# An attention layer on one core: output weights' sums made beside stage two's seven products, and residual additions moved from GpSimd to accumulating DMAs and VectorE

## The chip, the cores and the metric

The kernel runs on one core of a Trainium2 chip. The core has a matrix engine (TensorE, in the profile PE, with PEld for its weight loads) and three engines for elementwise work: VectorE (DVE), ScalarE (ACT) and GpSimd (POOL). A fifth, SyncE (SP), issues most of the DMAs; its queue is served in order. Each engine runs its instructions in program order and waits on semaphores for data from the others. The metric is the device time of one execution in microseconds, as the median of several runs.

## The reference

One pre-norm layer of a vision-like trunk, with 2048 tokens of width 1024 on a grid of 64 columns, 16 heads of 64, all in float32:

```python
h = rmsnorm(x, norm_0)
q, k, v, gate = split(h @ w_in_0, 4)                 # w_in_0: 1024 x 4096
o = neighbourhood_attention(q, k, v, rpb_0)          # 8 x 16 window, bias per head
x = x + (o * silu(gate)) @ w_out_0                   # w_out_0: 1024 x 1024
out = rmsnorm(x, norm_f)
```

The layer norm's factor is the inverse root of the mean square of each token; the same holds for the last norm. The window is cut at the edges of the grid.

## The kernel before

**Products.** TensorE multiplies 128x128 blocks with moving tiles of 128x512. To keep float32 accuracy, each operand is split into a high part (made on ScalarE by a copy to the matrix format) and a low part (the difference, made on VectorE), and a product is three matmuls: high by high, high by low, low by high. Where a 2x2 arrangement of blocks is at hand, the kernel uses Strassen's scheme with seven products in place of eight. It needs sums of quarters of both operands (S1 to S4 on one side, T1 to T4 on the other); a product is then 12 matmuls (4 blocks of the inner dimension by 3).

**Stages.** Stage one makes the norm's statistics, v for the first half of the tokens and q, k, gate for them by seven products. Stage two does the same for the second half: first the value projections (`values_of`, called by `pair`, line 834: 16 tiles of 24 matmuls), then nine units of seven products (`seven_products`, line 405; the order of the seven is 1, 6, 2, 7, 5, 4, 3). Then come 32 steps of attention (scores, softmax, transposes, values), with further projections and the first six tiles of output rows fed in between. Last come the other ten tiles of output rows, in five pairs by seven products (`rows_product` and `rows_by_seven`, lines 1440 and 1479), with the residual, the last norm and the stores.

**The output weights' sums.** For the last part the kernel needs T1 to T4 of `w_out`. They are made in stage two's value projections: for each of four row blocks k, `out_rows(k)` (line 886) issues four loads of 256 KB into OW, `out_sum` forms one difference on VectorE, and `out_split` makes high and low part of it and puts two stores to DRAM (`wod`) in the list of later stores. They stand in the table of `pair` calls (lines 919 to 937) as steps between two groups of matmuls. The same calls hold `w` (splits of the value weights), `lw` (loads of value weights, line 533), `v` (values out of PSUM), `block`, `t123`, `t4` and `form` (the other operands of stage two).

**What sets the order.** The program is written in the order in which each engine gets its instructions; there is no scheduler. `store(key, lag, f)` puts a piece of work into a list, and `due(n)`, called with each matmul, lets it out after `lag` matmuls. `ahead` in stage two makes high and low parts six products ahead. In the seven products of stage two a function `also(n, i)` is called after product i of the unit n (n counts up to 0 for the last unit). In the last part `LEAD` says how many products ahead the high and low parts are made, and `todo` says after which product of `seq` loads, sums and parts are issued. The weight tiles of value unit 1 use the buffers of unit 0's, and the landing tiles `raw` go round over six buffers.

**PSUM in the last part.** In a pair (n0, n1) of row tiles, products 1 and 2 share one bank, 6, 7 and 4 a second, 5 and 3 a third. Product 1 is copied out to `p` (U[m, 1]). After product 6, `u` = bank + p is the part of (n0, 1); after product 7, `u` = bank + p is that of (n1, 1); and p goes into (n1, 0). So product 7 waits until u of product 6 has read the bank, product 4 until u of product 7 has, and product 3 until the addition y of product 5 has. `add_rows` (line 1224) adds the bank to what stands in RES and leaves the square sums to ScalarE. What stands in RES for (n0, 1), (n1, 1) and (n1, 0) is u or p with the residual tile already added, by three additions on GpSimd (lines 1464 and 1468). The residual tiles are loaded by `load_rest_of` on SP's queue into `rbp` (three buffers) or `qp`.

Of the kernel before, what the change touches and what calls it, by code (L numbers as in the profile page):

```python
# [71 lines left out]
def build(ctx, tc, x, xr, xt, wg, rpb, last, w_out, n0, nf, masks, out):  # L72
# [728 lines left out]
    def stage_two():  # L801
# [8 lines left out]

        def also(n, i):
# [72 lines left out]
        OW = {}  # L884

        def out_rows(k):
            def g():
                for q, (r_, c_) in quarters.items():
                    OW[q] = kp([128, 960], F32, "ow")[:, :512] if r_ else ep([128, 512], F32, "ow")
                    nc.sync.dma_start(OW[q], w_out[(4 * r_ + k) * 128:(4 * r_ + k + 1) * 128, c_ * 512:c_ * 512 + 512])  # L890
            return g

        def out_sum(k, f):
            def g():
                a, b = {"T1": ("B12", "B11"), "T3": ("B22", "B12"), "T2": ("B22", "B11"), "T4": ("B21", "B22")}[f]
                o = OW[{"T1": "B11", "T3": "B12", "T2": "B22", "T4": "B21"}[f]]
                nc.vector.tensor_tensor(o, OW[a], OW[b], OP.subtract)
            return g

        def out_split(k, f):  # L900
            def g():
                o = OW[{"T1": "B11", "T3": "B12", "T2": "B22", "T4": "B21"}[f]]
                h, l = ev([128, 512], F32R, "oh"), ev([128, 512], F32R, "ol")
                split_to(h, l, o, None)
                for i, s in enumerate((h, l)):
                    store(("ow", f, k, i), 5, lambda i=i, s=s: nc.sync.dma_start(wod[f][:, k, i], s.bitcast(F32)))
            return g

# [7 lines left out]
        def o(k, *fs):  # L916
            return [(out_sum if f[0] == "+" else out_split)(k, "T" + f[-1]) for f in fs]

        pair(0, (8, 9), both(w(0, 3), lambda: spread_rstd(3)), both(lw(1, 0), block("B12", x12, 0, 1)),
             both(block("B12", x12, 2, 3), out_rows(0)), block("B22", x22, 0, 1))  # L920
        pair(0, (10, 11), both(v(0, 8, 9), block("B22", x22, 2, 3)), t123(0), t123(1), both(lw(1, 1), *o(0, "+1")))
# [4 lines left out]
        pair(1, (13,), both(v(1, 12), form("T2", x11, 2), *o(1, "=3")), both(form("T2", x11, 3), *o(1, "+2")), both(*o(1, "=2", "+4")),  # L926
             both(*o(1, "=4")))
        pair(1, (14,), both(v(1, 13), form("T3", x22, 0), out_rows(2)), form("T3", x22, 1), both(), both(*o(2, "+1")))
        pair(1, (15,), both(v(1, 14), lambda: ahead(-9, -1), *o(2, "=1", "+3")), both(form("T3", x22, 2), *o(2, "=3")),
             both(form("T3", x22, 3), *o(2, "+2")), both(*o(2, "=2", "+4")))  # L930
        pair(1, (8,), both(v(1, 15), lambda: ahead(-8, -1), *o(2, "=4")), both(t1(0), out_rows(3)), t1(1), lambda: ahead(-7, -1))
        pair(1, (9,), both(v(1, 8), t1(2), *o(3, "+1")), both(t1(3), *o(3, "=1")), both(lambda: ahead(-6, -1), *o(3, "+3")),
             both(form("T4", x21, 0), *o(3, "=3")))
        pair(1, (10,), both(v(1, 9), form("T4", x21, 1), *o(3, "+2")), both(form("T4", x21, 2), *o(3, "=2")),
             both(form("T4", x21, 3), *o(3, "+4")), both(*o(3, "=4")))
# [288 lines left out]
    def add_rows(n, j, ps):  # L1224
# [213 lines left out]

    def rows_product(m, P):
# [17 lines left out]
        elif P == 2:  # L1457
            add_rows(n0, 0, B[m, 2])
        elif P in (6, 7):
            U[m, P] = xp([128, 512], F32, "u")  # L1460
            nc.vector.tensor_tensor(U[m, P], B[m, P], U[m, 1], OP.add)
            to = (n0, 1) if P == 6 else (n1, 1)
            r = RES.pop(to)
            nc.gpsimd.tensor_tensor(U[m, P], U[m, P], r, OP.add)
            RES[to] = U[m, P]
            if P == 7:
                r = RES.pop((n1, 0))
                nc.gpsimd.tensor_tensor(U[m, 1], U[m, 1], r, OP.add)
                RES[n1, 0] = U[m, 1]
        elif P == 5:  # L1470
            add_rows(n1, 1, B[m, 5])
        elif P == 4:
            add_rows(n1, 0, B[m, 4])
            finish(n1)
        else:
            add_rows(n0, 1, B[m, 3])
            finish(n0)

    def rows_by_seven():
        for f, (r, c) in plain_of.items():  # L1480
            TF[f] = [(woh[4 * r + k, c], wol[4 * r + k, c]) for k in range(4)]
        E, LEAD = 3, 4
        seq = [(m, P) for P in (1, 2) for m in range(E)]
        seq += [(0, 6), (1, 6), (0, 7), (0, 5), (1, 7), (0, 4), (1, 5), (0, 3), (1, 4), (2, 6), (1, 3), (2, 7), (2, 5), (2, 4), (2, 3)]
        seq += [(m, P) for m in range(E, len(PAIRS)) for P in order7]
# [13 lines left out]
        for i, m, j, k in ((1, 0, 1, 0), (2, 1, 1, 0), (4, 0, 0, 1), (5, 0, 1, 1), (6, 1, 0, 1), (7, 1, 1, 1), (9, 2, 0, 1), (9, 2, 1, 0),  # L1499
                           (11, 2, 1, 1)):  # L1500
            on(i, load_rest_of, m, j, k)
        for m in range(E, len(PAIRS)):
            s = seq.index((m, 1))
            for d, f in ((-9, "A21"), (-8, "A22"), (-7, "A11"), (-6, "A12")):
# [214 lines left out]
```

## Time and profile before

| what | value |
|---|---|
| median of 3 runs | 1055.19 us (1054.54 to 1059.93) |
| the profiled execution's own time | 1056.66 us |
| its span, first to last instruction | 1054.9 us |
| mean granted clock of TensorE | 0.997 |
| DMA moved | 205.30 MB, mean 195 GB/s |
| stage two's value projections | about 326 to 420 us |
| stage two's seven products | about 420 to 590 us |
| the last five pairs of row tiles | 949.7 to 1048.9 us |

The span is the time on the core from the first to the last instruction; the execution's own time is a little longer. On the page, busy times of engines overlap. Rows of a timeline give start, duration, engine, line, operation, output and input, and in brackets the idle time before it and what ended that. In rows of windows each engine has its busy time and its count of instructions, then come the clock granted to TensorE (1.00 is full speed), the share of DMA engines' time and GB/s.

### The profile page before, as it was taken

Reading aid. Unit: us, or ns where it says so; the run is one execution under the profiler, and the core shown is the slowest. Engines: PE = TensorE matmul, PEld = TensorE weight load, DVE = VectorE, ACT = ScalarE, POOL = GpSimd, SP = SyncE. Lnnn points to the kernel's source line nnn. Section 1 sums busy time; section 2 is a strip of 40 time slices with the busy share of each in tenths; the row PEclk is TensorE's granted clock in tenths of the full one; section 3 lists DMA queues with packets and bytes.
Section 4 is the critical chain, followed back from the end, with each engine's and each line's share of the span. In section 5 each row is a group of like instructions: output and inputs, shape, how many; then the busy total and the mean of one; then the engine's idle time right before and its main releaser. Section 6 shows DMA issues by size and latency. Waiting matters only on the chain.

```text
span 1054.9 us, 20328 instructions
## 1 busy us (share of the span) xinstructions
PE 1039.0 (98%) x7256; PEld 850.1 (81%) x7256; DVE 743.2 (70%) x1601; ACT 558.4 (53%) x1305; POOL 278.1 (26%) x357
## 2 busy tenths in 40 slices
PE   9999999999999989999999999999999999999987
PEld 6888888887888868888888788888888787888776
DVE  5385657778897847655565666667777788777996
ACT  7545323344344435333333477788887877673433
POOL 0000231321221000000000477765565432420331
PEclk9999999999999999999999999999999999999999
DMA  9633444452637568434243787868877689899442
GB/s 312 226 100 100 140 145 129 134 151 96 195 119 211 168 230 293 126 108 132 80 145 121 237 246 218 260 199 279 249 237 247 186 269 312 277 352 354 148 172 80
DMA packets 133213, 205.30 MB, mean 195 GB/s; under 512 B 12216, under 2 KB 56504, under 8 KB 133112
## 3 DMA queue, kind: packets, MB, share of 16 engines
q1 hardware_dynamic: 132680, 203.61, 60.7%
q8 instruction: 57, 0.93, 0.4%
q10 hardware_dynamic: 432, 0.40, 0.1%
q14 instruction: 44, 0.36, 0.1%
HBM read 145.24 MB, written 58.72 MB: 193 GB/s over the span
## 4 chain that ended last, share of the span: by engine, by line
PE 89%; DVE 7%; issue 1%; ACT 1%; DMA 1%; POOL 0%; ACTq 0%; DVEq 0%
PE pp L438 36%; PE pv L562 12%; PE s L1063 8%; PE o L1170 8%; PE py L1451 7%; PE ph L1148 4%; PE pp L384 2%; PE po L1372 2%; PE po L1374 2%; PE pp L386 2%; PE pp L382 2%; PE po L1376 2%; DMA raw<-in_wg_dram 1%; DVE l L521 1%; DVE y L1291 1%
## 5 line engine op out<-in xcount | busy, mean ns | idle before, releaser
L438 PE MATMUL pp<-h,f 128*128 128x512 f32 x672 | 217.6, 389 | 0.0
L1077 ACT ACTIVATE x<-x,st 128x360 f32<-128x360 f32 (+5 forms) x256 | 151.2, 592 | 24.6 <-DVE st L1071 24.6
L438 PEld LDWEIGHTS pp<-h,f 128*128 128x128 f32 x672 | 126.1, 188 | 26.5 <-DVE f L421 0.3
L438 PE MATMUL pp<-t,f 128*128 128x512 f32 x558 | 141.7, 389 | 0.1
L1091 POOL TENSOR_SCALAR x<-x,st 128x480 f32<-128x480 f32 (+5 forms) x192 | 114.4, 613 | 94.1 <-DVE st L1082 91.8
L438 PE MATMUL pp<-l,f 128*128 128x512 f32 x336 | 130.7, 389 | 0.0
L458 POOL TENSOR_TENSOR tmp<-tmp,rb 128x512 f32<-128x512 f32 x36 | 58.4, 1622 | 271.1 <-DVE tmp L456 235.7
L1071 DVE CUSTOM_DVE_ANT_0 x<-s,em 128x360 f32<-128x360 f32 (+5 forms) x256 | 123.0, 535 | 0.3 <-PE s L1063 0.3
L438 PEld LDWEIGHTS pp<-t,f 128*128 128x128 f32 x558 | 104.7, 188 | 22.3 <-DVE u L451 0.6
L1031 POOL TENSOR_TENSOR em<-e,mk 128x264 f32<-128x264 f32 (+3 forms) x64 | 50.8, 825 | 266.2 <-DMA mk<-in_masks_dram 252.7
L421 DVE TENSOR_TENSOR f<-raw,f 128x512 fp32r<-128x512 f32 x105 | 76.5, 728 | 37.4 <-ACT f L420 37.3
L1063 PE MATMUL s<-kt,q 64*128 64x480 f32 (+5 forms) x512 | 95.5, 488 | 0.1
L562 PE MATMUL pv<-wh,h 128*128 128x512 f32 x256 | 90.0, 397 | 4.4 <-ACT wh L542 4.4
L1170 PEld LDWEIGHTS o<-pta,vt 120*64 120x64 f32 (+2 forms) x1792 | 80.9, 137 | 14.4 <-DVE st L1071 13.6
L562 PE MATMUL pv<-wl,h 128*128 128x512 f32 x256 | 89.8, 396 | 0.3 <-DVE wl L545 0.3
L562 PE MATMUL pv<-wh,l 128*128 128x512 f32 x256 | 89.5, 395 | 0.0
L1170 PE MATMUL o<-pta,vt 120*64 120x128 f32 (+5 forms) x1792 | 85.5, 253 | 0.5 <-DVE pta L1124 0.4
L420 ACT ACTIVATE f<-raw 128x512 fp32r<-128x512 f32 x105 | 63.8, 624 | 27.8 <-PE pp L438 12.5
L1063 PEld LDWEIGHTS s<-kt,q 64*128 64x128 f32 x512 | 64.7, 186 | 16.5 <-DVE pta L1124 2.1
L1124 DVE COPY pta<-ph 120x512 f32<-120x512 f32 (+5 forms) x96 | 56.9, 639 | 23.9 <-PE ph L1148 23.8
L438 PEld LDWEIGHTS pp<-l,f 128*128 128x128 f32 x336 | 63.1, 188 | 13.0
L1124 ACT ACTIVATE pta<-ph 120x512 f32<-120x512 f32 (+5 forms) x96 | 49.7, 557 | 37.1 <-PE ph L1148 36.4
(186 smaller groups left out, 1859.6 us busy)
## 6 DMA issues: line engine op xcount, KB each, us to landing
raw<-in_wg_dram SPq DMA_DIRECT2D x124, 256.0 KB, 4.7
row<-in_xr_dram SPq DMA_DIRECT2D x32, 256.0 KB, 4.3
vd<-v SPq DMA_DIRECT2D x32, 256.0 KB, 2.7
sgd<-sg SPq DMA_DIRECT2D x32, 256.0 KB, 2.4
q<-qd SPq DMA_DIRECT2D x32, 256.0 KB, 5.4
sgt<-sgd SPq DMA_DIRECT2D x32, 256.0 KB, 5.6
xr<-in_x_dram SPq DMA_DIRECT2D x32, 256.0 KB, 4.1
ogd<-og SPq DMA_DIRECT2D x32, 256.0 KB, 4.1
```

Of the source, the lines that this page charges most:

```text
L420: nc.scalar.activation(t[:, 0], src, AF.Copy)
L421: nc.vector.tensor_tensor(t[:, 1], src, t[:, 0].bitcast(F32), OP.subtract)
L438: nc.tensor.matmul(B[n, P], t[:, int(m == 2), c], x[k][int(m == 1)], start=P in (1, 6, 5) and k == 0 and m == 0, stop=k == 3 and m == 2, s ...
L458: nc.gpsimd.tensor_tensor(tmp, tmp, rb[c], OP.mult)
L562: nc.tensor.matmul(ps[t], a[:, o], b, start=k == 0 and m == 0, stop=k == NK - 1 and m == 2)
L1063: nc.tensor.matmul(pst[s], qt[a, qs], kt[a, :r1 - r0, c0:c1].rearrange("p r (s c) -> p s r c", c=8), start=True, stop=True)
L1071: nc.vector.tensor_tensor_reduce(X[i, C][s], pst[s], EM[p, ROW_TYPE[T], COL_TYPE[C], s], -1.0, 1e38, OP.add, OP.min, st[:, o:o + 1])
L1077: nc.scalar.activation(X[i, C][s], X[i, C][s], AF.Exp, bias=st[:, o:o + 1], scale=-1.0, accum_out=st[:, 4 + o:5 + o])
L1091: nc.gpsimd.tensor_scalar(X[i, C][s], X[i, C][s], st[:, o:o + 1], 1.0, op0=OP.mult, op1=OP.mult)
L1124: (nc.vector.tensor_copy if h else lambda o, i_: nc.scalar.activation(o, i_, AF.Copy))(t[:k, h, b * 512:b * 512 + w], banks_[b, h][:k, :w])
L1170: nc.tensor.matmul(to.rearrange("d (h q) -> d h q", q=64) if nq > 64 else to, vt[:k, strip, s * 64:s * 64 + 64], t[:k, h, at:at + 64] if n ...
L1451: nc.tensor.matmul(B[m, P], t[:, a, c], b, start=P in (1, 6, 5) and k == 0 and i == 0, stop=k == 3 and i == 2, skip_group_check=True)
```

## The change

There are two parts.

1. The output weights' sums leave the value projections of stage two. `out_rows`, `out_sum` and `out_split` are called from `also` in its seven products. Row block k starts behind the first product of unit 2k − 8 counted from the last, the eight steps follow from the third product on, one behind each product, and run into the next unit. The landing tiles are others: for odd k one tile of `mkp` and one of `kp`, for even k two of `rbp` and two of `kp`, where it was two of `ep` and two of `kp`.

2. In the last part the additions on GpSimd go. The residual of (n0, 1) is added to u, and that of (n1, 0) to p, by a DMA from x that accumulates into the tile, issued from GpSimd's queue (`add_rest`). That of (n1, 1) is added to u by VectorE from a loaded tile. Ten of the loads on SP's queue go with it. `LEAD` becomes 5, product 1 of pair 3 is drawn ahead of product 7 of pair 2, the loads for pair 3 start earlier, the remaining residual loads have other places, and for the last but one row tile the product with the last norm's weight is issued with the squares.

```diff
--- before.py
+++ after.py
@@ -808,7 +808,50 @@
+        def out_rows(k):
+            def g():
+                if k % 2:
+                    spot = mkp([128, 3, 512], F32, "ow")
+                    homes = [spot[:, i] for i in range(3)]
+                else:
+                    homes = [rbp([128, 512], F32, "ow") for _ in range(2)]
+                homes += [kp([128, 960], F32, "ow")[:, :512] for _ in range(4 - len(homes))]
...
+        sums_at = {}
+        for k in range(4):
+            n = 2 * k - 8
+            for i, f in enumerate([out_rows(k), None, *o(k, "+1", "=1", "+3", "=3", "+2", "=2", "+4", "=4")]):
+                if f:
+                    sums_at[n + i // 7, i % 7] = f
+
         def also(n, i):
+            if (n, i) in sums_at:
+                sums_at[n, i]()
...
-        pair(0, (12, 13), both(v(0, 10, 11), *o(0, "=1", "+3")), both(t123(2), *o(0, "=3", "+2")), both(t123(3), *o(0, "=2", "+4")),
-             both(t4(0, 1, 2, 3), lw(1, 2), *o(0, "=4")))
-        pair(0, (14, 15), both(v(0, 12, 13), w(1, 0), out_rows(1)), both(w(1, 1), lw(1, 3)), w(1, 2), w(1, 3))
-        pair(1, (12,), v(0, 14, 15), both(form("T2", x11, 0), *o(1, "+1")), both(form("T2", x11, 1), *o(1, "=1")), both(*o(1, "+3")))
...
+        pair(0, (12, 13), v(0, 10, 11), t123(2), t123(3), both(t4(0, 1, 2, 3), lw(1, 2)))
+        pair(0, (14, 15), both(v(0, 12, 13), w(1, 0)), both(w(1, 1), lw(1, 3)), w(1, 2), w(1, 3))
+        pair(1, (12,), v(0, 14, 15), form("T2", x11, 0), form("T2", x11, 1))
...
@@ -1250,11 +1260,10 @@
         def square():
             nc.scalar.activation(xr, y, AF.Square, scale=0.5 ** 0.5, accum_out=st[:, j:j + 1])
             squared[0] += 1
-
-        if n == tiles - 2:
-            w = ev([128, 512], F32, "yw")
-            nc.vector.scalar_tensor_tensor(w, y, 0.5 ** 0.5 / NF_SCALE, late["nf"][j], op0=OP.mult, op1=OP.mult)
-            Y[n][0][j] = w
+            if n == tiles - 2:
+                w = Y[n][0][j] = ev([128, 512], F32, "yw")
+                nc.vector.scalar_tensor_tensor(w, y, 0.5 ** 0.5 / NF_SCALE, late["nf"][j], op0=OP.mult, op1=OP.mult)
@@ -1436,6 +1445,9 @@
+    def add_rest(n, j, to):
+        nc.gpsimd.dma_start(to, x[n * 128:n * 128 + 128, 512 * j:512 * j + 512], accum_op=OP.add)
+
@@ -1460,12 +1472,14 @@
             to = (n0, 1) if P == 6 else (n1, 1)
-            r = RES.pop(to)
-            nc.gpsimd.tensor_tensor(U[m, P], U[m, P], r, OP.add)
-            RES[to] = U[m, P]
-            if P == 7:
-                r = RES.pop((n1, 0))
-                nc.gpsimd.tensor_tensor(U[m, 1], U[m, 1], r, OP.add)
+            if P == 6:
+                RES[to] = U[m, 6]
+                add_rest(n0, 1, U[m, 6])
+            else:
+                xr_ = RES.pop(to)
+                nc.vector.tensor_tensor(U[m, 7], U[m, 7], xr_, OP.add)
+                RES[to] = U[m, 7]
+                add_rest(n1, 0, U[m, 1])
                 RES[n1, 0] = U[m, 1]
@@ -1479,10 +1493,10 @@
-        E, LEAD = 3, 4
+        E, LEAD = 3, 5
         seq = [(m, P) for P in (1, 2) for m in range(E)]
-        seq += [(0, 6), (1, 6), (0, 7), (0, 5), (1, 7), (0, 4), (1, 5), (0, 3), (1, 4), (2, 6), (1, 3), (2, 7), (2, 5), (2, 4), (2, 3)]
-        seq += [(m, P) for m in range(E, len(PAIRS)) for P in order7]
+        seq += [(0, 6), (1, 6), (0, 7), (0, 5), (1, 7), (0, 4), (1, 5), (0, 3), (1, 4), (2, 6), (1, 3), (3, 1), (2, 7), (2, 5), (2, 4), (2, 3)]
+        seq += [(m, P) for m in range(E, len(PAIRS)) for P in order7 if (m, P) not in seq]
...
-            for d, j, k in ((-2, 0, 1), (-2, 0, 0), (-1, 1, 0), (0, 1, 1)):
-                on(s + d, load_rest_of, m, j, k)
+            on(s - 2, load_rest_of, m, 0, 0)
+            on(s, load_rest_of, m, 1, 1)
```

How this moves instructions stands in the order in which each engine gets them. On SP's queue in stage two, up to the last two loads of value weights (`raw`); `ow` are loads of output weights, `wodT` stores of split sums, `vd` stores of values. Before:

```order
L533 DMA raw<-in_wg_dram 128x512 x2
L906 DMA wodT_92<-oh 128x512
L906 DMA wodT_92<-ol 128x512
L890 DMA ow<-in_w_out_dram 128x512 x4
L397 DMA vd_83<-v 128x4x128 x2
L533 DMA raw<-in_wg_dram 128x512 x2
```

And now:

```order
L397 DMA vd_83<-v 128x4x128 x2
L533 DMA raw<-in_wg_dram 128x512 x2
L397 DMA vd_83<-v 128x4x128 x2
L533 DMA raw<-in_wg_dram 128x512 x2
L397 DMA vd_83<-v 128x4x128 x2
L397 DMA vd_84<-v 128x4x128 x2
```

The loads and stores of the sums are gone from between the weight loads; the rows are now stores of values and weight loads alone.

On VectorE in the last part, from the addition u of pair 2's product 7 on; `f` is a low part, `raw` and `s` are sums of the left operand, `y` an addition into the result. Before:

```order
L1461 TENSOR_TENSOR u<-py,p_11312 128x512
L1432 TENSOR_TENSOR s<-s,raw 128x512
L1426 TENSOR_TENSOR f<-raw,f 128x512
L1291 SCALAR_TENSOR_TENSOR y<-y,st_11360,acc_169 128x512
L1291 SCALAR_TENSOR_TENSOR y<-y,st_11360,acc_170 128x512
L1248 TENSOR_TENSOR y<-py,u 128x512
L1432 TENSOR_TENSOR raw<-raw 128x512
L1426 TENSOR_TENSOR f<-s,f 128x512
L1248 TENSOR_TENSOR y<-py,p_11312 128x512
```

And now:

```order
L1473 TENSOR_TENSOR u<-py,p_11309 128x512
L1480 TENSOR_TENSOR u<-u,xr 128x512
L1441 TENSOR_TENSOR raw<-raw 128x512
L1435 TENSOR_TENSOR f<-raw,f 128x512
L1258 TENSOR_TENSOR y<-py,u 128x512
L1435 TENSOR_TENSOR f<-raw,f 128x512
L1258 TENSOR_TENSOR y<-py,p_11309 128x512
```

The two scalings (line 1291) stand earlier now, ahead of this u, and the addition of the residual tile xr has come in behind it.

On GpSimd, all that it issues in the last part. Before:

```order
L1464 TENSOR_TENSOR u<-u,xr 128x512 x3
L1468 TENSOR_TENSOR p_11273<-p_11273,xr 128x512
L1464 TENSOR_TENSOR u<-u,xr 128x512
L1468 TENSOR_TENSOR p_11292<-p_11292,xr 128x512
L1464 TENSOR_TENSOR u<-u,xr 128x512 x2
L1468 TENSOR_TENSOR p_11312<-p_11312,xr 128x512
```

And now:

```order
L1449 DMA u<-in_x_dram 128x512 x2
L1449 DMA p_11269<-in_x_dram 128x512
L1449 DMA p_11288<-in_x_dram 128x512
L1449 DMA u<-in_x_dram 128x512
L1449 DMA p_11309<-in_x_dram 128x512
```

Three additions a pair have become two DMAs a pair; the rows shown are those of pairs 0 to 2, and pairs 3 and 4 go on in the same way.

More of the change, by code (lines that the diff above doesn't have):

```diff
@@ L882, in form @@
             return g
[L884 to L907, printed above, removed]
         def t1(*ks):
@@ L914, in t1 @@
             return g
[L916 to L921, printed above, removed]
-        pair(0, (12, 13), both(v(0, 10, 11), *o(0, "=1", "+3")), both(t123(2), *o(0, "=3", "+2")), both(t123(3), *o(0, "=2", "+4")),
-             both(t4(0, 1, 2, 3), lw(1, 2), *o(0, "=4")))
@@ L929, in stage_two @@
[L929 to L933, printed above, removed]
@@ L934, in stage_two @@
-        pair(1, (10,), both(v(1, 9), form("T4", x21, 1), *o(3, "+2")), both(form("T4", x21, 2), *o(3, "=2")),
-             both(form("T4", x21, 3), *o(3, "+4")), both(*o(3, "=4")))
+        pair(0, (8, 9), both(w(0, 3), lambda: spread_rstd(3)), both(lw(1, 0), block("B12", x12, 0, 1)), block("B12", x12, 2, 3),
+             block("B22", x22, 0, 1))
+        pair(0, (10, 11), both(v(0, 8, 9), block("B22", x22, 2, 3)), t123(0), t123(1), lw(1, 1))
+        pair(0, (12, 13), v(0, 10, 11), t123(2), t123(3), both(t4(0, 1, 2, 3), lw(1, 2)))
@@ new lines, in stage_two @@
+        pair(0, (14, 15), both(v(0, 12, 13), w(1, 0)), both(w(1, 1), lw(1, 3)), w(1, 2), w(1, 3))
+        pair(1, (12,), v(0, 14, 15), form("T2", x11, 0), form("T2", x11, 1))
+        pair(1, (13,), both(v(1, 12), form("T2", x11, 2)), form("T2", x11, 3))
+        pair(1, (14,), both(v(1, 13), form("T3", x22, 0)), form("T3", x22, 1))
+        pair(1, (15,), both(v(1, 14), lambda: ahead(-9, -1)), form("T3", x22, 2), form("T3", x22, 3))
+        pair(1, (8,), both(v(1, 15), lambda: ahead(-8, -1)), t1(0), t1(1), lambda: ahead(-7, -1))
@@ L936, in stage_two @@
+        pair(1, (9,), both(v(1, 8), t1(2)), t1(3), lambda: ahead(-6, -1), form("T4", x21, 0))
+        pair(1, (10,), both(v(1, 9), form("T4", x21, 1)), form("T4", x21, 2), form("T4", x21, 3))
         pair(1, (11,), both(v(1, 10), lambda: ahead(-5)), lambda: ahead(-4), both(lambda: ahead(-3), lambda: ahead(-2)),
@@ L1498, in rows_by_seven @@
             on(i, load_rows_of, 2, f)
-        for i, m, j, k in ((1, 0, 1, 0), (2, 1, 1, 0), (4, 0, 0, 1), (5, 0, 1, 1), (6, 1, 0, 1), (7, 1, 1, 1), (9, 2, 0, 1), (9, 2, 1, 0),
-                           (11, 2, 1, 1)):
-            on(i, load_rest_of, m, j, k)
         for m in range(E, len(PAIRS)):
-            s = seq.index((m, 1))
-            for d, f in ((-9, "A21"), (-8, "A22"), (-7, "A11"), (-6, "A12")):
+            s = seq.index((m, 6)) - 1
+            for d, f in ((-12, "A11"), (-10, "A21"), (-9, "A22"), (-7, "A12")) if m == E else \
+                    ((-9, "A21"), (-8, "A22"), (-7, "A11"), (-6, "A12")):
                 on(s + d, load_rows_of, m, f)
@@ L1507, in rows_by_seven @@
                 on(s + d, sum_rows, m, f)
[L1508 to L1509 removed]
+            on(s - 2, load_rest_of, m, 0, 0)
+            on(s, load_rest_of, m, 1, 1)
+        for i, m in ((5, 0), (7, 1), (11, 2)):
+            on(i, load_rest_of, m, 1, 1)
         for i, s in enumerate(seq):
```

24 lines of the change are left out of this document (21 added, 3 removed).

## The prediction

> **What bounds the kernel now.** I began with the page's busy times and the chain that ended last, then asked the trace who TensorE (PE) waited for.
>
> ```profile
> span 1054.9 us, 20328 instructions
> ...
> PE   1039.0 (98%) x7256; PEld 850.1 (81%) x7256; DVE 743.2 (70%) x1601; ACT 558.4 (53%) x1305; POOL 278.1 (26%) x357
> ...
> PE 89%; DVE 7%; issue 1%; ACT 1%; DMA 1%; POOL 0%; ACTq 0%; DVEq 0%
> ```
>
> TensorE is busy for 1039.0 of 1054.9 us, and the change leaves its matmuls as they are in number and shape. A gain can only come from the gaps in it, and from the tail behind its last matmul. The table of waits on PE has, beside the start-up:
>
> ```profile
> PE pv L562 <- ACT wh L542: 4.4, 2, 3.7
> PE py L1451 <- DVE y L1248: 2.2, 1, 2.2
> ...
> PE py L1451 <- DVE u L1461: 0.4, 1, 0.4
> ...
> PE pv L562 <- DVE wl L545: 0.3, 1, 0.3
> PE py L1451 <- ACT f L1425: 0.3, 1, 0.3
> ```
>
> Two places matter: one stop of 3.7 us in a value projection (pv), and three of together 2.9 us in the output rows (py). By stage (columns: PE, PEld, DVE, ACT, POOL busy with their counts, clock, DMA):
>
> ```profile
> 325.00:420.00 95.00, 91.02 (x394) 74.54 (x392) 64.95 (x100) 40.28 (x73) 2.70 (x2) 0.98 0.70 222
> 420.00:590.00 170.00, 170.00 (x751) 140.68 (x750) 99.32 (x157) 56.63 (x100) 6.54 (x8) 1.00 0.42 132
> ...
> 949.70:1048.90 99.20, 96.21 (x420) 78.43 (x420) 80.83 (x140) 37.04 (x87) 23.45 (x15) 1.00 0.53 189
> ```
>
> 325 to 420 us are stage two's value projections, where the output weights' sums are made now; 420 to 590 are its seven products, where they go: PE never waits there, and VectorE (DVE) is busy 99.32 of 170 us.
>
> **The stop in the value projections.** Timeline of PE, ACT and SP around it:
>
> ```profile
> 364.61 2.19 ACT L542 ACTIVATE wh<-raw 128x512 fp32r<-128x512 f32 x4
> 366.45 1.94 SPq L890 DMA_DIRECT2D ow<-in_w_out_dram  x4
> 369.61 1.37 SPq L533 DMA_DIRECT2D raw<-in_wg_dram  x2
> 373.88 0.39 PE L562 MATMUL pv<-wh,l 128*128 128x512 f32 x1
> 376.75 1.15 ACT L542 ACTIVATE wh<-raw 128x512 fp32r<-128x512 f32 x2 [8.27 <-DMA raw<-in_wg_dram]
> 377.95 0.51 PE L562 MATMUL pv<-wh,h 128*128 128x512 f32 x1 [3.67 <-ACT wh L542]
> 378.76 0.50 PE L562 MATMUL pv<-wl,h 128*128 128x512 f32 x1 [0.30 <-DVE wl L545]
> ...
> 378.76 41.09 PE pv L562 x173
> ...
> 949.68 31.75 PE py L1451 x140
> ```
>
> The last two weight loads of value unit 1 stand on SP's in-order queue behind four loads of the output weights. They go out at 369.61, land at 376.75, and PE restarts at 377.95. The undisturbed pitch of a matmul is 31.75 / 140 = 0.2268 us. The matmul after 373.88 was due at 374.11 and came at 377.95: 3.84 us. The next was due at 378.18, came at 378.76: 0.58. The 173 from there take 41.09 us instead of 39.24: 1.85 more. Why:
>
> ```profile
> 378.00:380.00 2.00, 1.70 (x5) 1.15 (x6) 1.28 (x3) 1.90 (x4) 0.00 (x0) 0.81 0.36 110
> 380.00:382.00 2.00, 2.00 (x7) 1.54 (x6) 1.85 (x4) 1.21 (x3) 0.00 (x0) 0.50 0.51 152
> 382.00:384.00 2.00, 2.00 (x9) 1.67 (x8) 1.90 (x4) 1.58 (x3) 0.00 (x0) 0.83 0.68 262
> ```
>
> The granted clock fell to 0.50 behind the gap. The stop costs 3.84 + 0.58 + 1.85 = **6.3 us**, not the 3.7 that the table of waits shows.
>
> **What the move does there.** Between the stores of the values and those two loads nothing else is left on SP: the four loads (1.94 us of issue) and the stores of the split sums go. SP came to the four loads at 366.45, so the two can go out by then at the latest.
>
> ```profile
> raw<-in_wg_dram SPq DMA_DIRECT2D x124, 256.0 KB, 4.7
> L897 DVE TENSOR_TENSOR ow<-ow 128x512 f32<-128x512 f32 x16 | 11.0, 685 | 7.1 <-DMA ow<-in_w_out_dram 7.1
> 280.00:300.00 20.00, 20.00 (x90) 16.58 (x89) 19.69 (x27) 7.00 (x12) 4.84 (x3) 1.00 0.38 121
> ```
>
> At the median of 4.7 us they land at 371.2; at the 7.1 us of the disturbed case (376.75 − 369.61) at 373.6. Split and restart took 377.95 − 376.75 = 1.2 us, so PE could go on at 372.4 to 374.8, and needs them at 374.11: a wait of 0 to 0.7 us. I take 0, since the megabyte loaded just ahead of them is gone. Term one: **−6.3 us**.
>
> Where the sums go, VectorE gets 16 subtractions at 0.685 us and 16 low parts of the same shape, 22 us on top of 99.32 of 170; ACT gets 16 high parts, and SP 16 loads and 32 stores. The cover is PE's own work: VectorE stood at 19.69 of 20 us in stage one at 280 to 300 us with PE at 20.00. A sum that waits for its load holds up the additions from PSUM queued behind it on VectorE; those are needed one product (12 × 0.2268 = 2.72 us) later. The sum stands two products (5.4 us) behind its load, which takes about 4.7. Bounds: nothing, or, if each of the four groups came late by 1 us past that, 4 us; without VectorE's spare time it would be the whole 22. I take 0.
>
> **The output rows.** 420 matmuls at 0.2268 are 95.25 us; the stretch from 949.70 to 1048.90 took 99.20. Lost: 3.95 us, most of it here:
>
> ```profile
> 1002.53 1.62 POOL L1464 TENSOR_TENSOR u<-u,xr 128x512 f32<-128x512 f32 x1 [4.49 <-ACT f L1425]
> 1002.91 1.79 DVE L1426 TENSOR_TENSOR f<-raw,f 128x512 fp32r<-128x512 f32 x1
> 1004.62 2.43 DVE L1291 SCALAR_TENSOR_TENSOR y<-y,st,acc 128x512 f32<-128x512 f32 x2
> 1006.98 0.68 DVE L1248 TENSOR_TENSOR y<-py,u 128x512 f32<-128x512 f32 x1
> ...
> 1005.16 0.39 PE L1451 MATMUL py<-sixths,f 128*128 128x512 f32 x1
> 1007.80 0.47 PE L1451 MATMUL py<-woh,f 128*128 128x512 f32 x1 [2.25 <-DVE y L1248]
> ```
>
> Product 3 accumulates into product 5's bank, so it waits for the addition y that reads product 5. That addition stands behind a low part f of 1.79 us and two scalings of 2.43, all beside a POOL addition. Over the stage:
>
> ```profile
> L1426 DVE TENSOR_TENSOR f<-raw,f 128x512 fp32r<-128x512 f32 x18 | 15.4, 866 | 0.1
> L1291 DVE SCALAR_TENSOR_TENSOR y<-y,st,acc 128x512 f32<-128x512 f32 x18 | 14.7, 859 | 0.0
> L1426 DVE TENSOR_TENSOR f<-s,f 128x512 fp32r<-128x512 f32 x15 | 11.8, 789 | 1.5 <-ACT f L1425 1.5
> ...
> L1432 DVE TENSOR_TENSOR s<-raw 128x512 f32<-128x512 f32 x5 | 4.8, 959 | 4.1 <-DMA raw<-ogd 4.1
> ```
>
> Against 0.68 to 0.69 us undisturbed, these groups carry 18 × 0.18 + 18 × 0.17 + 15 × 0.10 + 5 × 0.27 = 9.2 us of delay. With the 15 POOL additions gone it goes too; five additions of 0.68 come, 3.4 us. VectorE drops from 80.8 to about 75 us. The new addition stands between product 7's and product 5's, ahead of y, so y is ready some 0.7 us later than otherwise, against 2.72 us of slack. Putting pair 3's product 1 ahead of pair 2's product 7 gives VectorE one more product before the place that stalled. Low parts made five products ahead instead of four, and later residual loads on a queue with seven fewer of them, I cost at nothing: what covers them is four products, 10.9 us. Bounds: none or all of 3.95; I take **−3.6**, leaving 0.35 for the small waits on f and u.
>
> **The accumulating DMAs.** The trace of before has none. The nearest rows are the loads of the same x tiles on SP's queue (issue to landing, min, median, max):
>
> ```profile
> DMA to landing us min/median/max: 2.8/4.1/6.0
> ...
> 1041.12 0.69 DVE L1461 TENSOR_TENSOR u<-py,p 128x512 f32<-128x512 f32 x1
> ...
> 1046.25 0.69 DVE L1248 TENSOR_TENSOR y<-py,p 128x512 f32<-128x512 f32 x1 [1.27 <-PE py L1451]
> ...
> 1048.92 0.76 DVE L1234 TENSOR_TENSOR y<-py,u 128x256 f32<-128x256 f32 x2
> ```
>
> From below 2.8 us, a plain load at its quickest; from above 6.0 + 1.62 (the slowest, and POOL's addition as the price of adding) = 7.6. I take the middle, 5.2. The one on p is the tight one: it may start when u of product 7 has read p (1041.12 + 0.69 = 1041.8) and must be in place for y of product 4 at 1046.25, 4.4 us later. In the last pair everything from that y to the last addition at 1048.92 runs back to back on VectorE, so lateness there goes straight into the end. Term three: 5.2 − 4.4 = **+0.8** (0 to 3.2). The one on u6 has five products, 13.6 us: free. [...]
>
> **Sum.** −6.3 − 3.6 + 0.8 = −9.1 us. Span 1054.9 → 1045.8; the profiled execution's own 1056.66 us → 1047.6. The median of the runs, 1055.19, lies 1.5 under that execution; taken from it the sum gives **1046.1 us**.
>
> **Rivals.** 0.5% is 5.3 us, about what a measurement of this kernel tells from no change: faster is under 1049.9, slower over 1060.5.
>
> A, the stop in the output rows stays: the five new VectorE additions sit ahead of the very y that PE waits for. Against it: the row of 1.79 us is 0.68 without POOL. Price 3.6: 1049.7. Chance 0.10.
>
> B, the DMAs land near 7.6 us. VectorE then waits 3.2 us at product 4 in pairs 2, 3 and 4; in pairs 2 and 3 the additions behind it may be late by one product, so PE loses about 1 us in each; in the last pair 3.2 instead of 0.8 goes into the end: 1046.1 + 2 + 2.4 = 1050.5. Chance 0.09.
>
> C, writing the DMAs' orders on POOL holds VectorE as its additions do. Ten instead of fifteen holds of 1.1 us (1.79 − 0.68) leave a third of the relief; half of the 3.6 is lost and a hold is added to the last landing: 1046.1 + 1.8 + 1.1 = 1049.0. Chance 0.06. [...]
>
> D, the sums bring no gain in stage two, because the last weights come late anyway or the four groups of sums stop PE for as much: 1046.1 + 6.3 = 1052.4. Chance 0.05.
>
> E, slower: an accumulating DMA reads both sides one after the other, 2 × 6.0 = 12 us. VectorE is held 7.6 us at product 4; less one product's slack PE loses 4.9 in pairs 2 and 3 each and 2.2 in pair 0, which has three products between; the end 6.8 beyond the term above: 1046.1 + 9.8 + 2.2 + 6.8 = 1064.9. It eats the gain from L with 2(L − 7.1) + (L − 5.2) = 9.1, L = 9.5 us. For it: nothing shows the second read. Against it: twice the slowest load. Chance 0.04.
>
> The forecast has 0.66, by itself 1044.2 to 1048.5 (all of 6.3 and 3.95 gained and no tail; or a tail of 3.2). The range reaches over A, C and most of B: 1044.2 to 1050.6. Faster: 0.64 of the forecast, 0.06 of A, 0.05 of C, 0.04 of B: 0.79. Slower: E, 0.04. The rest, 0.17, is no change.
>
> **What would show it.** Stage two: no wait on wh L542 over 1 us, clock 1.00 throughout, the value projections 6.3 us shorter, 420 to 590 us still without a wait on PE. Output rows: no VectorE instruction of 1.8 us, 420 matmuls within 95.6 us, the chain there on PE alone. Tail: y of product 4 in the last pair waits for an accumulating DMA by 0 to 1 us. Wrong would be a wait on DMA at each pair's product 4, PE stops in the seven products of stage two behind ow, or a tail over 9 us from last matmul to end.

## The result, and the profile after

| what | before | after |
|---|---|---|
| median | 1054.84 us (1054.54 to 1059.93) | 1046.35 us (1045.78 to 1047.92) |
| the profiled execution's own time | 1056.66 us | 1047.92 us |
| its span | 1054.9 us | 1046.1 us |
| mean granted clock of TensorE | 0.997 | 0.999 |

The ratio is 0.9911, with a 95% interval of 0.9887 to 0.9934: 0.9% faster, clear of the noise. Both medians are of five executions, and the profiled one of the changed kernel is its slowest. The prediction was 1046.1 us, faster. The page's span, busy times and chain:

```profile
span 1046.1 us, 20290 instructions
...
PE 1035.6 (99%) x7256; PEld 848.4 (81%) x7256; DVE 736.4 (70%) x1606; ACT 558.0 (53%) x1305; POOL 263.0 (25%) x352
...
PE 95%; DVE 2%; DMA 1%; ACT 1%; issue 0%; SPq 0%; ACTq 0%; DVEq 0%
```

VectorE's share of the chain has gone from 7% to 2%. From the table of waits on PE, in us in total, times, and the longest:

```profile
PE py L1463 <- ACT f L1434: 1.5, 1, 1.5
...
PE pv L562 <- ACT wh L542: 0.7, 1, 0.7
```

The stop of 3.7 us on wh and the one of 2.2 us on y are gone; a stop of 1.5 us in the output rows is new. The table's only other rows, 1.2 us on z at the start and 0.4 on pta in the attention, stand in it before as well. (The 0.7 on wh belongs to the first unit of values at the start, not to the place that stalled.) The three stages in windows, columns as before:

```profile
325.00:420.00 95.00, 95.00 (x420) 78.59 (x420) 51.44 (x80) 34.87 (x63) 2.01 (x2) 1.00 0.42 116
420.00:590.00 170.00, 170.00 (x754) 140.15 (x753) 116.21 (x184) 62.84 (x112) 6.85 (x8) 1.00 0.60 197
942.54:1040.00 97.46, 95.92 (x420) 78.39 (x420) 75.23 (x146) 37.42 (x87) 8.82 (x10) 1.00 0.64 196
```

In the first, PE is busy for 95.00 of 95.00 us at full clock, where it had 91.02 at 0.98. In the second, VectorE has taken the sums, 116.21 us for 99.32, and PE still never waits. In the third, VectorE fell from 80.83 to 75.23 us and GpSimd from 23.45 to 8.82, but 420 matmuls still need 97.46 us, not 95.25. From the two chains and timelines, stage by stage:

| stage | before | after | difference |
|---|---|---|---|
| up to stage two's value projections | 325.98 | 325.29 | −0.7 |
| value projections | 93.87 | 87.74 | −6.1 |
| seven products to the end of attention | 529.8 | 529.4 | −0.4 |
| the last five pairs | 99.20 | 97.47 | −1.7 |
| last matmul to the end | 6.02 | 6.15 | +0.1 |
| span | 1054.9 | 1046.1 | −8.8 |

The first row is not the change's: in the profiles of this study that stage ends between 323.0 and 326.0 us with the same instructions, so below stages are compared, not spans. The chain of waits shows the value projections and the seven products as unbroken stretches of matmuls (start, length):

```profile
328.66 84.37 PE pv L562 x372
413.03 171.36 PE pp L438 x756
```

84.37 / 372 = 0.2268, the undisturbed pitch. The last weight loads are in time now: SP issues them at 362.32, and ACT's high part waits for PE to release the buffer, not for a DMA.

```profile
362.32 0.95 SPq L533 DMA_DIRECT2D raw<-in_wg_dram  x2
...
369.09 1.15 ACT L542 ACTIVATE wh<-raw 128x512 fp32r<-128x512 f32 x2 [1.56 <-PE pv L562]
```

The new stop in the output rows, first on VectorE and POOL (timelines), then in the chain of waits:

```profile
997.04 0.86 POOL L1449 DMA_DIRECT2D p<-in_x_dram  x1 [7.27 <-DVE u L1473]
```

```profile
999.19 0.68 DVE L1435 TENSOR_TENSOR f<-raw,f 128x512 fp32r<-128x512 f32 x1
1002.68 0.69 DVE L1258 TENSOR_TENSOR y<-py,p 128x512 f32<-128x512 f32 x1 [2.81 <-issue]
```

```profile
1005.64 0.69 DVE y L1258
...
1006.93 1.32 DVE y L1300 x2
...
1009.04 0.62 ACT f L1434
...
1009.74 30.22 PE py L1463 x132
```

Read together: the DMA that adds the residual to p of pair 2 goes out at 997.04. VectorE has done the low part f at 999.87, and the last matmul of product 4 ends at 1000.12, so y of product 4 could be formed then. VectorE stands idle for 2.81 us until p is complete at 1002.68, 5.6 us behind the issue. The profile calls that "issue" because it has no releaser for it. Behind y everything on VectorE is late: the sum s, the next additions, the scalings and the statistics of the last norm. ACT takes the square root of these (st) ahead of the high part f that pair 3's product 7 needs, and so PE, far from the place of the wait, stops until 1009.74. (The trace puts the gap of 0.33 us ahead of the y at 1005.64 down to PE. VectorE's own order explains nearly all of that y's lateness: where pair 2's p is added by VectorE, below, the same y follows product 4's y after 2.64 us, here after 2.96.) In pair 3 VectorE waits 0.69 us in the same way and PE doesn't stop for it, and in the last pair the wait isn't there, since y waits for PE:

```profile
1019.21 0.69 DVE L1258 TENSOR_TENSOR y<-py,p 128x512 f32<-128x512 f32 x1 [0.69 <-issue]
...
1037.26 0.69 DVE L1258 TENSOR_TENSOR y<-py,p 128x512 f32<-128x512 f32 x1 [1.30 <-PE py L1463]
```

The accumulating DMAs by issue and landing (the list of DMA issues, then the tile p alone):

```profile
p<-in_x_dram POOLq DMA_DIRECT2D x5, 256.0 KB, 4.6
...
DMA to landing us min/median/max: 4.0/4.6/5.6
```

### The profile page after: what moved, and what is told of

Its sections match the earlier page's. It is cut to its first block, busy times and chain, and to the rows that moved or that the text cites. A ratio compares the mean times of both kernels' runs of the same rounds, so it can differ in the third digit from the quotient of the medians.

```text
span 1046.1 us, 20290 instructions
## 1 busy us (share of the span) xinstructions
PE 1035.6 (99%) x7256; PEld 848.4 (81%) x7256; DVE 736.4 (70%) x1606; ACT 558.0 (53%) x1305; POOL 263.0 (25%) x352
## 4 chain that ended last, share of the span: by engine, by line
PE 95%; DVE 2%; DMA 1%; ACT 1%; issue 0%; SPq 0%; ACTq 0%; DVEq 0%
PE pp L438 37%; PE pv L562 17%; PE py L1463 9%; PE s L1073 8%; PE o L1180 8%; PE ph L1158 4%; PE pp L384 2%; PE pp L386 2%; PE pp L382 2%; PE po L1381 2%; PE po L1383 2%; PE po L1385 2%; DMA sgt<-sgd 1%; DVE f L421 0%; DMA vt<-vd 0%
```

## The experiments

The runs, with the median and the ratio to the kernel before, each taken on the same chip as that kernel.

| kernel | median us | ratio, 95% interval |
|---|---|---|
| the sums alone | 1049.59 | 0.994 [0.9924, 0.9957] |
| the output rows alone | 1053.0 | 0.9976 [0.9967, 0.9986] |
| before, weight loads ahead of the sums' loads | 1053.73 | 0.998 [0.9968, 0.9992] |
| changed, one product between DMA and use | 1044.34, again 1045.1 | 0.9893 [0.9876, 0.991], 0.9894 [0.9875, 0.9913] |
| changed, pair 2's p by VectorE | 1044.79 | 0.9891 [0.9875, 0.9907] |
| changed, GpSimd's additions for the DMAs | 1049.07 | 0.9931 [0.9915, 0.9946] |
| changed, once more | 1046.57 | 0.9908 [0.9891, 0.9924] |
| changed, product 1 of pair 3 in its old place | 1045.31 | 0.9906 [0.9887, 0.9925] |
| changed, more VectorE work beside the sums | 1049.0 | 0.9943 [0.9923, 0.9962] |

### Each part by itself

The sums alone: the changed kernel with the last part as it was before.

```diff
-        E, LEAD = 3, 5
+        E, LEAD = 3, 4
...
-                add_rest(n0, 1, U[m, 6])
...
+            r = RES.pop(to)
+            nc.gpsimd.tensor_tensor(U[m, P], U[m, P], r, OP.add)
```

> The first part of the change alone (the sums beside the seven products; the output rows as before). If the stop in stage two's value projections came from the two weight loads queued behind the output weights' loads, the value projections shorten from 93.9 to about 87.7 us with the clock at 1.00, the output rows keep their 99.2 us, and the median is about 6.1 to 6.3 us under before (near 1048.6). If the two parts need each other (the sums' new place disturbs the output rows through buffers that both use), the output rows take over 100 us and the gain is under 5 us.

```profile
326.38 84.37 PE pv L562 x372
410.75 171.36 PE pp L438 x756
```

```profile
PE py L1461 <- DVE y L1258: 2.2, 1, 2.2
PE py L1461 <- ACT f L1435: 1.7, 1, 1.7
```

The chain shows value projections and seven products to the hundredth as in the changed kernel; so the gain in stage two doesn't hang on the other part. The table of waits keeps the stop on y and has a second one of 1.7 us, on ACT's f. In this profile the output rows take 100.8 us, 1.6 more than before, so on that point the other branch of the expectation came true; why that stop came up isn't shown. The median is 5.8 us below the kernel before on that chip (1055.39).

The output rows alone: the changed kernel with the sums back in the value projections.

```diff
-            if (n, i) in sums_at:
-                sums_at[n, i]()
...
+        pair(0, (14, 15), both(v(0, 12, 13), w(1, 0), out_rows(1)), both(w(1, 1), lw(1, 3)), w(1, 2), w(1, 3))
```

> The second part alone (the output rows as changed; the sums as before). If the parts add up, the stop of 3.8 us near 374 us stays with its slow clock, the output rows take about 97.5 us instead of 99.2, and the median is 1.5 to 2.5 us under before (near 1052.8). If the second part only helps because the first one shifts it, the output rows stay at 99 us or more and the median is that of before.

```profile
PE pv L562 <- ACT wh L542: 3.4, 1, 3.4
PE py L1453 <- ACT f L1424: 1.5, 1, 1.5
```

The stop of stage two is back and the new one of 1.5 us stays: it belongs to the second part. This part gains 2.4 us by the medians, and 5.8 + 2.4 = 8.2, against 8.5 for both: within the noise the two add up, though the output rows of the first run were longer.

### Was it the order of SP's queue?

The kernel before, with the four loads of w_out one step later, behind the last two weight loads; nothing else moved.

```diff
-        pair(0, (14, 15), both(v(0, 12, 13), w(1, 0), out_rows(1)), both(w(1, 1), lw(1, 3)), w(1, 2), w(1, 3))
+        pair(0, (14, 15), both(v(0, 12, 13), w(1, 0)), both(w(1, 1), lw(1, 3), out_rows(1)), w(1, 2), w(1, 3))
```

> The kernel before with one thing changed: the four loads of the second row block of output weights are issued behind the last two weight loads of value unit 1 and not ahead of them. All sums stay in the value projections. If the queue's order makes the stop, it falls from 3.8 us to 1 us or less, the clock stays above 0.9, and the median is 5 to 6.3 us under before (near 1049). If the sums' work on VectorE and ScalarE makes the weights' splits late, the stop stays at 2.5 us or more and the gain is under 2.5 us.

Timelines of SP, ACT and PE:

```profile
365.15 1.36 SPq L533 DMA_DIRECT2D raw<-in_wg_dram  x2
366.57 2.20 SPq L890 DMA_DIRECT2D ow<-in_w_out_dram  x4
```

```profile
371.60 0.63 ACT L542 ACTIVATE wh<-raw 128x512 fp32r<-128x512 f32 x1 [5.47 <-DMA raw<-in_wg_dram]
372.96 0.63 ACT L542 ACTIVATE wh<-raw 128x512 fp32r<-128x512 f32 x1 [0.73 <-DMA raw<-in_wg_dram]
```

```profile
373.65 0.49 PE L562 MATMUL pv<-wh,h 128*128 128x512 f32 x1 [1.75 <-ACT wh L542]
```

This was a miss for both theories. The loads go out 4.5 us earlier than before (365.15 for 369.61), but the second lands 372.96 − 365.15 = 7.8 us behind the first's issue, with a megabyte issued right behind them. The stop falls from 3.67 to 1.75 us, not to none. So the queue's order is about half of that stop. In the other half the loads, though early, land late; that the sums' loads beside them are the cause is likely, but no run moved these away and left the rest. Moving the sums away removes both halves. The gain of 1.7 us by the medians is less than the stop gave back. The profile, which is of the slowest of this kernel's eleven executions, shows what took it there: a stop of 1.7 us in the seven products (pp on ACT's f), and output rows of 101.7 us for 99.2, with a stop of 1.2 us on ACT's f and a clock slowed to 0.50 (last section).

### Is the hold of VectorE what stops PE in the output rows?

One product put between the DMA's issue and its use: product 1 of pair 3 goes behind product 5 of pair 2 instead of ahead of product 7.

```diff
-        seq += [..., (2, 6), (1, 3), (3, 1), (2, 7), (2, 5), (2, 4), (2, 3)]
+        seq += [..., (2, 6), (1, 3), (2, 7), (2, 5), (3, 1), (2, 4), (2, 3)]
```

> The changed kernel with product 1 of pair 3 put between products 5 and 4 of pair 2 instead of ahead of its product 7, so that three products (8.2 us) and not two lie between u of product 7 and the addition y of product 4. If the accumulating DMA on p (4.0 to 5.6 us from issue to landing) holds VectorE and through it makes the stop of 1.5 us near 1008 us, VectorE's wait of 2.8 us at that addition falls under 0.5 us, the stop goes, the output rows take about 96 us, and the median is 1 to 1.6 us under the changed kernel's 1046.35 (near 1045). If VectorE's load there is the cause (new addition, scalings), the stop stays at 1 us or more somewhere in pairs 2 and 3 and the median is within 0.5 us of the changed kernel.

```profile
941.10 95.44 PE py L1463 x420
```

```profile
998.34 0.69 DVE L1435 TENSOR_TENSOR f<-raw,f 128x512 fp32r<-128x512 f32 x1 [0.65 <-ACT f L1434]
998.95 0.69 DVE L1258 TENSOR_TENSOR y<-py,p 128x512 f32<-128x512 f32 x1
```

In the chain all 420 matmuls stand in one row, 95.44 us against 95.25 at the pure pitch, and on VectorE y follows f without a wait. Beside the changed kernel on the same chip it took 1045.1 (1044.71 to 1045.57) against 1046.57 us (1046.01 to 1047.52): 1.5 us, the size of the stop.

The other way out is to take that one DMA away: the residual of pair 2's p is loaded into a tile and added by VectorE.

```diff
+                if m == 2:
+                    xr_ = RES.pop((n1, 0))
+                    nc.vector.tensor_tensor(U[m, 1], U[m, 1], xr_, OP.add)
+                else:
+                    add_rest(n1, 0, U[m, 1])
```

> The changed kernel with one of its ten accumulating DMAs undone: in pair 2 alone the residual is added to p by VectorE from a tile loaded on SP's queue. If that DMA's landing time is what holds VectorE, its wait of 2.8 us at y of product 4 in pair 2 goes, the stop of 1.5 us on TensorE goes with it though VectorE has one addition of 0.7 us more, and the output rows take 96 us or less (before it 97.5): about 1.5 us under the changed kernel. If VectorE's amount of work is the cause, the added 0.7 us makes the stop longer, 1.5 to 2.2 us.

```profile
996.54 0.68 DVE L1484 TENSOR_TENSOR p<-p,xr 128x512 f32<-128x512 f32 x1
...
999.54 0.69 DVE L1258 TENSOR_TENSOR y<-py,p 128x512 f32<-128x512 f32 x1
```

The timeline has no idle time ahead of y, and the stop at pair 3's product 7 is gone. At 0.68 us the addition on VectorE is cheaper here than a DMA that costs it 2.81 us of waiting. Another stop of 0.95 us, at pair 0's product 7 on ACT's f, stands in this profile. The changed kernel's second profile repeats both the wait (2.76 us) and the stop (1.4 us). So by two different edits that both end the hold of VectorE, the stop goes; that the hold made it is shown.

Last, product 1 of pair 3 back where it was before, behind pair 2.

> The changed kernel with product 1 of pair 3 back in its old place, behind pair 2's last product. Theory (VectorE is held at pair 2's product 4 because the accumulating DMA on p has only product 5 between its issue and its use; where product 1 of pair 3 stands ahead of product 7 makes no difference to that): VectorE still waits 2 to 3.5 us at y<-py,p of pair 2, and PE still stops, 1 to 3 us in all in py; 1045 to 1049 us. Rival 1 (the prediction's: the draw ahead gives VectorE a product of room): PE stops grow by a product's share, 2.7 us more than in the changed kernel, near 1049 us. Rival 2 (the draw ahead itself makes the stop, by needing operands earlier): no stop in py, near 1044.5 us as where it stands between products 5 and 4.

```profile
991.56 0.86 POOL L1449 DMA_DIRECT2D p<-in_x_dram  x1 [3.96 <-DVE u L1473]
```

```profile
997.12 0.68 DVE L1258 TENSOR_TENSOR y<-py,p 128x512 f32<-128x512 f32 x1
```

```profile
995.32 0.68 DVE L1258 TENSOR_TENSOR y<-py,u 128x512 f32<-128x512 f32 x1
```

```profile
996.14 0.47 PE L1463 MATMUL py<-woh,f 128*128 128x512 f32 x1 [0.91 <-DVE y L1258]
```

My theory fell in part. I expected VectorE to wait 2 to 3.5 us here too, as the same products lie between the DMA and its use, and it waits not at all. Between the issue and the y of product 4 there are 5.6 us instead of 2.83 (999.87 − 997.04), as VectorE itself is later with what stands between, and no DMA on a tile p took more than 4.5 us in this profile. What PE loses is 0.9 us at product 3, behind y of product 5. That is the place that stalled for 2.25 us before the change, and that doesn't stall in the changed kernel. So the prediction's reading, that the draw ahead gives VectorE room before that place, is right there; the size that the expectation gave to it, 2.7 us more of stops than in the changed kernel, did not come. The rival that the draw itself makes the stop is right too, for pair 3's product 7: the draw shortens the time that the DMA has. Without it PE loses 0.9 us at one place, with it 1.5 at the other. By the medians nothing can be told between this kernel and the changed one.

### Are the DMAs worth it?

The changed kernel's order and its VectorE addition, with GpSimd's additions in place of the ten DMAs and the residual loads back.

```diff
-                add_rest(n0, 1, U[m, 6])
+                xr_ = RES.pop(to)
+                nc.gpsimd.tensor_tensor(U[m, 6], U[m, 6], xr_, OP.add)
...
-                add_rest(n1, 0, U[m, 1])
+                xr_ = RES.pop((n1, 0))
+                nc.gpsimd.tensor_tensor(U[m, 1], U[m, 1], xr_, OP.add)
```

> The changed kernel's order of products, lead and new VectorE addition, with the two accumulating DMAs of each pair replaced by GpSimd additions from loaded tiles, as before the change. If GpSimd's additions are what stretched VectorE's instructions, rows of 1.8 us come back (about ten GpSimd additions, 6 to 9 us in all), TensorE stops for 1.5 to 4 us in pairs 2 and 3, and the median is 0 to 3 us over the changed kernel. If the new order alone brought the gain in the output rows, they take 97.5 us or less, as with the DMAs.

By line, for the last part (count, busy us, mean ns), and the longest wait on PE:

```profile
L1300 DVE SCALAR_TENSOR_TENSOR y<-y,st,acc 128x512 f32<-128x512 f32 x18 | 14.7, 861 | 0.0
...
L1441 DVE TENSOR_TENSOR raw<-raw 128x512 f32<-128x512 f32 x5 | 5.6, 1120 | 0.0
```

```profile
PE py L1463 <- DVE u L1473: 2.7, 1, 2.7
```

The sums raw take 1120 ns in the mean, where the changed kernel has 682, and the scalings 861, where it has 745: 18 × 0.116 + 5 × 0.438 = 4.3 us of VectorE's time from these two groups alone. PE gets a stop of 2.7 us, the five pairs take 100.5 us, 3.0 more than with the DMAs, and the median is 2.5 us above the changed kernel's on that chip. So it is the DMAs, not the new order, that take the delay off VectorE.

### How much room do the seven products have?

Each of the 16 low parts of the sums is formed three times, the same values into the same tile: 32 instructions more.

```diff
                 split_to(h, l, o, None)
+                for _ in range(2):
+                    nc.vector.tensor_tensor(l, o, h.bitcast(F32), OP.subtract)
```

> The changed kernel with each of the 16 low parts of the output weights' sums formed three times on VectorE, the same values into the same tile, so 32 more instructions of 0.685 us, 22 us, in stage two's seven products: VectorE goes from 116 to about 138 of 170 us there. Theory (the sums lie in VectorE's spare time, and 54 us of it are left): no wait on PE between 413 and 584 us, seven products 171.4 us as before, time as the changed kernel, 1045 to 1048 us. Rival (the sums pass only because each is short: what queues behind them on VectorE, the additions out of PSUM, has one product of 2.7 us of room, and 1.4 us more per sum eats it): PE stops by up to 1.4 us at each of 16 places, 5 to 22 us longer, 1051 us or more.

Windows of that kernel, the whole stage and 7 us within it, and the longer of two stops on PE:

```profile
410.77:585.75 174.98, 173.44 (x758) 141.43 (x757) 137.48 (x216) 62.76 (x113) 7.32 (x8) 1.00 0.61 195
...
470.00:477.00 7.00, 6.67 (x30) 5.19 (x28) 6.93 (x12) 2.80 (x5) 0.00 (x0) 1.00 0.70 241
```

```profile
477.51 0.98 PE L438 MATMUL pp<-t,f 128*128 128x512 f32 x3 [0.84 <-DVE u L451]
```

The stage grew by 3.5 us for 22 us of VectorE work: 174.98 us, where by the same reading of the timeline the changed kernel has 171.52 (412.87 to 584.39). Neither theory had it: nothing was too low, 5 us too high. VectorE has 37 us to spare over the stage, yet it is busy for 6.93 of 7 us ahead of the stop. An average over a stage doesn't cover a burst: as the change has it the work passes without a wait on PE, and twice the added work does not.

## Why the prediction was right, and where it wasn't

The forecast was −9.1 us of span, the measurement −8.8 (by the medians 8.5 us, from 1054.84). Its terms did not come out alike.

- **The stop in stage two, −6.3 predicted, −6.1 measured.** The mechanism held: the loads go out early, PE waits 0, the clock stays at 1.00. The stop was counted with what followed it, 3.84 + 0.58 + 1.85, and not at the 3.7 of the table of waits; the measured gain bears that out. I gave two reasons, the queue and the megabyte that is gone. The loads-first run shows the queue's order as about half of the stop; that the megabyte makes the other half is argued, not shown.
- **The sums beside the seven products, 0 predicted, 0 measured** (171.36 us, no wait on PE). The run with more VectorE work shows that the cover ends somewhere within another 22 us.
- **The output rows, −3.6 predicted, −1.7 measured.** This is the term that was mis-sized. VectorE's relief came as worked out: 80.8 to 75.2 us, "about 75" predicted, low parts at 683 to 686 ns in the mean instead of 866 and 789. The next step, that drawing pair 3's product 1 ahead "gives VectorE one more product before the place that stalled", held for product 3: PE doesn't wait there, and waits 0.9 us without the draw. The step that failed is the 0.35 us left "for the small waits on f and u": it has no price for VectorE's wait on the DMA at y of product 4 in pair 2, to which the draw leaves 2.83 us, nor for the stop of 1.5 us that PE makes of it at pair 3's product 7.
- **The accumulating DMAs, +0.8 predicted, +0.1 measured at the end.** The guess of 5.2 us for one lies within the 4.0 to 5.6 measured, and the bounds of 2.8 and 7.6 held; over all runs the DMAs took 3.7 to 7.6 us, the longest one on a u in the run with pair 2's p by VectorE. But I took the time available, 4.4 us, from the last pair alone and charged the lateness only there. In the last pair the DMA was in time, and the 0.1 is not its; in pair 2, with 2.83 us available and a landing of 5.6, it was 2.81 late. The budget should have been read at each place of use, in the new order.

The errors of the last two terms, 1.9 too much gain and 0.7 too much loss, offset each other in part, and two rows of the stage table that the forecast has at nothing, the first and the one up to the end of attention, gave 1.1. That the sum comes within 0.3 us is luck. (The prediction also counts seven residual loads fewer on SP's queue; the lists of DMAs have 32 before and 22 after. Nothing hangs on it.)

Of the rivals, B had the mechanism: VectorE waiting at product 4, and PE losing about 1 us later in each of pairs 2 and 3. It came true in one pair, with a DMA of 5.6 us instead of 7.6 and a loss of 1.5. A, the stop on y staying, did not come; the stop that is there has another cause. C, that writing the DMAs' orders holds VectorE, is refuted: no tensor addition of VectorE (128x512) is stretched beside the ten DMAs, their groups' means are 682 to 692 ns. With GpSimd's additions in the DMAs' place the sums raw took 1120 ns against 682. D fell with stage two. E, 12 us a DMA, fell with the 4.0 to 5.6 us.

What stays open: why the DMA on pair 2's p took 5.6 us in the changed kernel (5.5 in its second profile, and 5.9 with the output rows alone, which have the same order) and 4.5 to 4.7 with the other two orders. In the changed kernel SP issues two stores, three loads of sums' operands and a residual tile between 995.5 and 1000.2 us, around its issue at 997.04; in the kernel with one product between, that DMA goes out at 992.06, ahead of the same burst. That the burst delays it was not tried by itself.

The version with one product between is faster than both kernels, by 1.5 us beside the changed one on the same chip, with no wait on PE in the output rows.

## What to carry to other kernels

When an addition by an engine becomes an accumulating DMA, the engine is relieved but a landing time takes its place, 3.7 to 7.6 us in these runs: work out, at each place of use and in the new order, how long it is from the last writer's end to the first reader, and put a product between where it is shorter. Price a stop by all that follows from it, the slowed clock too, not by the table of waits (6.1 us here for 3.7 in the table); and when a load is late behind others, ask whether its place in the queue or something beside it makes it late: here a new order cured only half, 3.67 to 1.75 us. Don't take a stage's average for cover: here VectorE, with 37 us to spare over the stage, was busy for 6.93 of 7 us, and PE stopped behind it.

## What was not expected of the hardware

How long a stop was did not by itself say, in these runs, whether TensorE was slowed behind it. Behind a stop of 2.25 us in the output rows the granted clock stays at 1.00 in the kernel before, and behind one of 2.25 us at the same place it falls to 0.50 in the loads-first run. The 180 matmuls from there take 41.09 and 42.67 us. Rows of the chain and windows behind the stop, of the kernel before and then of the loads-first run:

```profile
1007.80 41.09 PE py L1451 x180
```

```profile
1008.00:1010.00 2.00, 2.00 (x10) 1.61 (x10) 2.00 (x4) 1.45 (x4) 0.00 (x0) 1.00 0.80 234
```

```profile
1004.83 42.67 PE py L1451 x180
```

```profile
1006.00:1008.00 2.00, 2.00 (x6) 1.51 (x6) 1.50 (x5) 1.20 (x4) 0.00 (x0) 0.50 0.85 252
```

The stops of 2.67 us (GpSimd's additions) and 3.4 us (the output rows alone) also take it to 0.50:

```profile
998.00:1000.00 2.00, 2.00 (x5) 1.63 (x6) 2.00 (x2) 0.00 (x0) 1.71 (x1) 0.50 0.91 249
```

```profile
376.00:378.00 2.00, 2.00 (x5) 1.54 (x5) 1.59 (x3) 1.11 (x3) 0.00 (x0) 0.50 0.87 262
```

The seven longest stops behind the start of the kernel, with the clock in the windows behind each (us; for the sums alone it is the mean of the profiled execution, where the 180 matmuls behind the stop take 41.06 us):

| stop | from, to | length | clock behind it |
|---|---|---|---|
| before, value projections | 374.27, 377.95 | 3.67 | 0.50 |
| output rows alone, value projections | 371.51, 374.94 | 3.43 | 0.50 |
| GpSimd's additions, output rows | 995.32, 997.99 | 2.67 | 0.50 |
| loads first, output rows | 1002.58, 1004.83 | 2.25 | 0.50 |
| before, output rows | 1005.55, 1007.80 | 2.25 | 1.00 |
| sums alone, output rows | 997.68, 999.93 | 2.25 | 1.00 |
| loads first, value projections | 371.90, 373.65 | 1.75 | 1.00 |

The clock fell behind the stops of 2.67 us and more and stayed behind the one of 1.75 us; at 2.25 us it fell once and stayed twice. Nor does the slow time go by the length: behind the stop of 3.67 us the windows of 2 us from 378 us on have 0.81, 0.50 and 0.83, behind the one of 3.43 us those from 374 us on have 0.50, 0.50, 0.50 and 0.81. What sorts the cases is not shown: no run moved a stop and left the rest as it was. The profile models where a matmul ends, so the lengths are not exact.

In the full windows of 2 us behind these stops PE has 5 to 7 matmuls at 0.50 and 10 or 11 at 1.00, and counts as busy for all of the 2 us in both. So the slow clock is a part of the 6.1 us that a stop of 3.7 us cost (the 173 matmuls behind it took 41.09 us, 1.85 more than at 0.2268 each), and the row of busy time alone doesn't show it.
